# The first norm of the sample rows on ScalarE: row squares and row scaling moved off VectorE

## Chip, cores and metric

The kernel runs on one core of a Trainium2 chip. The metric is device time in microseconds (us), from the start to the end of one execution of the program. The core's engines are TensorE (PE; weight loads are listed as PEld), VectorE (DVE), ScalarE (ACT), GpSimd (POOL) and SyncE (SP), which issues the transfers here. Each engine works through a queue of its own in order; they wait for each other by semaphores.

## What is computed

The reference is one layer of an encoder with two parallel head groups, run for a prompt of 512 rows and a sample of 1024 rows with the same weights, 1024 channels wide, all in float32:

```python
h = _rmsnorm(x, norm_attn_g[l])            # the norm that is changed, for the sample's rows
z = h @ w_in[l]                            # 1024 -> 1792: q, k, v of the attention, ca, cb of the convolution
a_out = _window_attn(q, k, v, bias, band, attn_sink[l])      # 8 heads, 2 kv heads, |q-k| <= 128
c = ca * jax.nn.sigmoid(cb)
c = _dwconv(c, conv_dw_w[l], conv_dw_b[l])                   # 31 taps
c = jax.nn.silu(_layernorm(c, conv_ln_g[l], conv_ln_b[l]))
x = x + jnp.concatenate([a_out, c], axis=-1) @ w_out[l]
h = _rmsnorm(x, norm_ffn_g[l])
u = _dwconv(h @ w_up[l], ffn_dw_w[l], ffn_dw_b[l])           # 3 taps
x = x + (jax.nn.silu(u[..., :D_FF]) * u[..., D_FF:]) @ w_down[l]
# _rmsnorm(x, g): x * rsqrt(mean(x * x over the channels) + 1e-6) * g; once more at the end
```

## The kernel before

**Tiling.** Rows are handled in tiles of 128 rows by 1024 channels, four of which make a block of 512 rows: block 0 is the prompt, blocks 1 and 2 are the sample. Every matmul operand is split into a rounded part and a rest (`split`, lines 140 to 145: a cast on ScalarE, line 143, and a subtraction on GpSimd, line 144), and each product is three matmuls (lines 250, 251, 253; line 257 is the late form of the third).

**The first norm.** `make_h1(nt)` takes the four x tiles of block `nt`, calls `norm_in_place` on each, and then `transposed`. `norm_in_place` sums the squares of each row, alternately on ScalarE (even tiles, line 196) and on VectorE (odd tiles, line 198), lets GpSimd make the factor rsqrt(mean + eps) of it (`rstd_of`, lines 127 and 128), and scales the tile in place on VectorE (line 201). `transposed` has TensorE transpose the four tiles chunk by chunk (line 209) into a PSUM bank; ScalarE takes the rounded part out of it (line 211) and VectorE the rest (line 212), after which the bank is free.

**What runs beside it.** The prompt's projections (`step(i, 0)`) go through 14 chunks of 128 columns of `w_in`; for each, `want_raw` loads the weights (line 137) and `want_w` splits them. `evac` takes the result out of its bank: for a `cb` chunk a tanh on ScalarE (line 314), for the `ca` chunk after it a multiplication with that tanh on VectorE (line 323). A finished pair gives one channel group of the convolution, `conv_items`: a first tap on VectorE (line 289), 26 more for the prompt (line 293), and four taps on ScalarE (lines 282 and 285) that GpSimd adds up (line 286); line 301 joins the two. The small constants come in through TensorE transposes and VectorE copies (lines 176, 416 to 420); the bias table goes from VectorE (line 434) to DRAM (lines 436 and 438).

`make_h1(0)` runs first of all. `make_h1(1)` is queued in `side` at the fourth chunk and `make_h1(2)` at the sixth; `tick` takes a step from `side` at a pace while the prompt's projections go on.

**What sets the order.** The order of the Python calls gives priorities only. The scheduler of the Tile framework deals the instructions of each engine into a queue by a simulated timeline, so a change of one instruction's engine can move others. `tc.issue_after(marks[...])` keeps block 1's norm behind the last bank evacuation of block 0. From the sample's feed-forward part on (line 1202), TensorE's order is the written one.

**Buffers.** `sb` hands out named slots of SBUF (15 of 4 KiB, `q`, for x tiles and weights), `banks` eight PSUM banks `a`, `u`, `b`, `c`. A transfer into a slot waits until the last reader of the slot is done.

Of the kernel before, what the change touches and what calls it, by code (L numbers as in the profile page):

```python
# [12 lines left out]
AF = mybir.ActivationFunctionType  # L13
# [83 lines left out]
def tile_hybrid_encoder(ctx: ExitStack, tc: tile.TileContext, xs, rel_bias, norm_attn_g, w_in,  # L97
                        attn_sink, conv_dw_w, conv_dw_b, conv_ln_g, conv_ln_b, w_out, norm_ffn_g,
                        w_up, ffn_dw_w, ffn_dw_b, w_down, norm_final_g, onehot, outs):
    nc = tc.nc  # L100
# [11 lines left out]
    def sm(n):  # L112
        return sb.tile([n])
# [12 lines left out]
    def rstd_of(ss, n, out):  # L126
        nc.gpsimd.tensor_scalar(out, ss, 1.0 / n, EPS, op0=ALU.mult, op1=ALU.add)
        nc.gpsimd.tensor_tensor(out, out, nhalf[:], op=ALU.pow)
# [60 lines left out]
    lng, lnb, fb = vecs[:, 20:24], vecs[:, 24:28], vecs[:, 28:72]  # L189


    def norm_in_place(x, k):
        ss, rs = sm(1), sm(1)
        junk = sb.tile([D], BF16, 2)
        if k % 2 == 0:
            nc.scalar.activation(junk[:], x[:], AF.Square, accum_out=ss[:])
        else:
            nc.vector.tensor_tensor_reduce(out=junk[:], in0=x[:], in1=x[:], scale=1.0, scalar=0.0,
                                           op0=ALU.mult, op1=ALU.add, accum_out=ss[:])
        rstd_of(ss[:], D, rs[:])  # L200
        nc.vector.tensor_scalar_mul(x[:], x[:], rs[:])

    marks = []

    def transposed(xn, g, h):
        for kc in range(KC):
            pt = bank("turn")
            for i in range(4):
                nc.tensor.transpose(pt[:, i * P:(i + 1) * P], xn[i][:, kc * P:(kc + 1) * P], ident[:])
            hi, lo = sb.tile([NT], F32R), sb.tile([NT], F32R)  # L210
            ia = nc.scalar.activation(hi[:], pt[:], AF.Identity, scale=g[:, kc:kc + 1])
            iv = nc.vector.scalar_tensor_tensor(lo[:], pt[:], g[:, kc:kc + 1], hi[:].bitcast(F32),  # L212
                                                op0=ALU.mult, op1=ALU.subtract)
            h.append((hi, lo))
            marks.append((ia.ins, iv.ins))
            yield 0.0
# [154 lines left out]
    def make_h1(nt):  # L371
        xt = xq.pop(nt)
        for k, x in enumerate(xt):
            if nt == 1:
                with tc.issue_after(marks[KC - 1][0]), tc.issue_after(marks[KC - 1][1]):
                    norm_in_place(x, k)
            else:
                norm_in_place(x, k)
            if nt:
                yield 0.0  # L380
        h1[nt] = []
        yield from transposed(xt, gA, h1[nt])
# [12 lines left out]
    for _ in make_h1(0):  # L395
        pass
# [45 lines left out]
    for i in range(npr):  # L442
        if i == 3:
            side.append(make_h1(1))
        if i == 5:
            xq[2] = [load_x(GR[1], 4 + i) for i in range(4)]
            side.append(make_h1(2))
        if i == 1:
            constants()
            bbd = bias_to_dram()  # L450
        want_raw(i + 2)
        want_w(i + 1)
        step(i, 0)
        ws.pop(i)
# [1115 lines left out]
```

## Time and profile before

| | us |
|---|---|
| median of three runs | 1566.0 (1565.88 to 1571.18) |
| the profiled execution | 1563.92 |
| its span, first to last instruction | 1562.1 |
| TensorE busy | 1519.2 |
| VectorE busy | 1200.5 |
| ScalarE busy | 799.2 |
| GpSimd busy | 729.5 |

The mean granted TensorE clock of that execution is 0.998. Busy times are sums over one engine; matmuls overlap in their pipeline, so a stretch in which TensorE is listed as fully busy is one without a gap. In the rows of the timeline the first number is the start and the second the duration; what stands in brackets is the time that the engine was idle before the row, and the instruction that ended it. Tile names carry the slot's letter: `q<-q` on line 201 is an x tile scaled in place.

### The profile page before, as it was taken

The numbers are of one execution on the slowest core, as the hardware profiler recorded it, in microseconds if no ns is written. First come the engines' busy times: TensorE is split into PE (matmuls) and PEld (weight loads), VectorE is DVE, ScalarE is ACT, GpSimd is POOL, SyncE is SP. The second block draws the span as 40 slices with busy tenths as digits, with TensorE's granted clock in tenths as the row PEclk, the third lists the DMA queues.
The fourth block names the chain that finished last, engine by engine and source line by source line (L and its number), as shares of the span: only waits on it lengthen the run. The fifth ranks groups of instructions, "written<-read, shape, count | busy, mean of one in ns | idle before, by whom it ended". The sixth has DMA issues, their size and how long they took to land. (4 is left out here: it accounts for less than half of the span.)

```text
span 1562.1 us, 20200 instructions
## 1 busy us (share of the span) xinstructions
PE 1519.2 (97%) x6909; PEld 1234.5 (79%) x6909; DVE 1200.5 (77%) x1731; ACT 799.2 (51%) x1426; POOL 729.5 (47%) x559
## 2 busy tenths in 40 slices
PE   8899899999998999999999999999999999999998
PEld 6787788887886778888877887888888878788886
DVE  7999868638989996756675768777777777877795
ACT  4634566335565655656554455444444445544364
POOL 7651344238576676656653324555555554000135
PEclk9999999999999999999999999999999999999999
DMA  7573246446331333333657222333333332694642
GB/s 229 157 201 95 87 118 165 130 133 166 108 117 64 108 108 109 99 97 95 212 164 230 82 68 78 111 102 101 101 102 102 101 102 101 206 354 144 219 142 108
DMA packets 209771, 207.62 MB, mean 133 GB/s; under 512 B 11156, under 2 KB 150748, under 8 KB 209541
## 3 DMA queue, kind: packets, MB, share of 16 engines
q1 hardware_dynamic: 209669, 206.35, 42.0%
q8 instruction: 54, 0.88, 0.2%
q14 instruction: 48, 0.39, 0.1%
HBM read 158.84 MB, written 48.51 MB: 133 GB/s over the span
## 5 line engine op out<-in xcount | busy, mean ns | idle before, releaser
L144 POOL TENSOR_TENSOR q<-q,q 128x1024 fp32r<-128x1024 f32 x72 | 175.0, 2436 | 68.8 <-ACT q L143 33.8
L921 POOL TENSOR_TENSOR q<-q,q 128x512 fp32r<-128x512 f32 x82 | 114.0, 1401 | 155.9 <-ACT q L1031 151.4
L250 PE MATMUL u<-h,q 128*128 128x512 f32 x400 | 158.5, 396 | 3.6 <-DVE h L775 2.8
L251 PE MATMUL u<-h,q 128*128 128x512 f32 x400 | 158.6, 396 | 0.6 <-DVE h L212 0.6
L253 PE MATMUL u<-h,q 128*128 128x512 f32 x384 | 151.9, 396 | 2.2 <-POOL q L144 2.2
L1045 PE MATMUL w<-h,q 128*128 128x512 f32 x372 | 147.4, 396 | 3.1 <-ACT h L1126 1.7
L1047 PE MATMUL w<-h,q 128*128 128x512 f32 x372 | 145.9, 392 | 0.6 <-POOL q L921 0.6
L293 DVE SCALAR_TENSOR_TENSOR c<-c,cvw,c 128x512 f32<-128x512 f32 x184 | 138.1, 750 | 2.4
L1046 PE MATMUL w<-h,q 128*128 128x512 f32 x350 | 137.6, 393 | 0.0
L143 ACT CAST q<-q 128x1024 fp32r<-128x1024 f32 x72 | 75.6, 1050 | 77.5 <-POOL q L144 44.6
L918 POOL TENSOR_TENSOR q<-q,q 128x1024 f32<-128x1024 f32 x8 | 23.8, 2989 | 182.9 <-DVE q L918 171.2
L250 PE MATMUL b<-h,q 128*128 128x512 f32 x256 | 102.1, 399 | 2.9 <-DVE d L323 2.9
L1354 PE MATMUL w<-h,h 128*128 128x512 f32 x264 | 103.8, 393 | 0.0
L1356 PE MATMUL w<-h,h 128*128 128x512 f32 x264 | 103.6, 392 | 0.0
L921 DVE TENSOR_TENSOR h<-h,h 128x512 fp32r<-128x512 f32 (+1 forms) x128 | 92.3, 764 | 11.4 <-ACT h L925 9.2
L251 PE MATMUL b<-h,q 128*128 128x512 f32 x256 | 100.7, 393 | 0.0
L253 PE MATMUL b<-h,q 128*128 128x512 f32 x256 | 100.5, 393 | 0.0
L1355 PE MATMUL w<-h,h 128*128 128x512 f32 x244 | 95.9, 393 | 0.0
L921 POOL TENSOR_TENSOR c<-q,c 128x512 fp32r<-128x512 f32 x46 | 71.0, 1557 | 51.8 <-ACT c L1031 51.8
L250 PEld LDWEIGHTS u<-h,q 128*128 128x128 f32 x400 | 75.6, 189 | 20.4 <-DVE h L775 3.3
L925 ACT CAST h<-h 128x512 fp32r<-128x512 f32 x101 | 58.7, 618 | 59.4 <-DVE h L921 27.0
L251 PEld LDWEIGHTS u<-h,q 128*128 128x128 f32 x400 | 75.5, 189 | 16.4 <-DVE h L212 1.6
(457 smaller groups left out, 4278.8 us busy)
## 6 DMA issues: line engine op xcount, KB each, us to landing
q<-in_w_up SPq DMA_DIRECT2D x88, 512.0 KB
h<-in_w_down SPq DMA_DIRECT2D x90, 256.0 KB
ga<-q SPq DMA_DIRECT2D x64, 256.0 KB
h<-ga SPq DMA_DIRECT2D x57, 256.0 KB
q<-in_w_in SPq DMA_DIRECT2D x28, 512.0 KB
q<-in_x_sample SPq DMA_DIRECT2D x15, 512.0 KB
h<-qsd SPq DMA_DIRECT2D x24, 256.0 KB
q<-ga SPq DMA_DIRECT2D x20, 256.0 KB
```

Source lines behind the costliest of these rows:

```text
L144: (nc.vector if dve else nc.gpsimd).tensor_tensor(lo[:], raw[:], hi[:].bitcast(F32), op=ALU.subtract)
L250: nc.tensor.matmul(out, whi[:, kc, :], hi[:], start=(kc == 0), stop=False)
L251: nc.tensor.matmul(out, whi[:, kc, :], lo[:], start=False, stop=False)
L253: nc.tensor.matmul(out, wlo[:, kc, :], hi[:], start=False, stop=(kc == KC - 1))
L293: nc.vector.scalar_tensor_tensor(acc[:], src(t), w(t), acc[:], op0=ALU.mult, op1=ALU.add)
L921: (eng or nc.vector).tensor_tensor(out, a, b, op=ALU.subtract)
L1045: nc.tensor.matmul(out, whi[:, s], hi[:], start=(start and c == 0), stop=False, **go)
L1046: nc.tensor.matmul(out, whi[:, s], lo[:], start=False, stop=False, **go)
L1047: nc.tensor.matmul(out, wlo[:, s], hi[:], start=False, stop=(stop and c == 3), **go)
L1354: nc.tensor.matmul(out, sh[:, c], th[:], start=(p == 0), stop=False)
L1355: nc.tensor.matmul(out, sh[:, c], tl[:], start=False, stop=False)
L1356: nc.tensor.matmul(out, sl[:, c], th[:], start=False, stop=(p == NPAIR - 1))
```

## The change

For the sample's blocks (`nt` 1 and 2) all four squares of a block are ScalarE activations, and the scaling of each tile is a ScalarE activation with the row factor as its scale. The prompt's block (`nt` 0) keeps both engines and the scaling on VectorE. The reduction's scratch tile, the row factor on GpSimd, the transposes and the loads are as they were. In numbers: four squares and eight scalings move from VectorE to ScalarE.

```diff
-    def norm_in_place(x, k):
+    def norm_in_place(x, k, first):
         ss, rs = sm(1), sm(1)
         junk = sb.tile([D], BF16, 2)
-        if k % 2 == 0:
+        if k % 2 == 0 or not first:
             nc.scalar.activation(junk[:], x[:], AF.Square, accum_out=ss[:])
         else:
             nc.vector.tensor_tensor_reduce(out=junk[:], in0=x[:], in1=x[:], scale=1.0, scalar=0.0,
                                            op0=ALU.mult, op1=ALU.add, accum_out=ss[:])
         rstd_of(ss[:], D, rs[:])
-        nc.vector.tensor_scalar_mul(x[:], x[:], rs[:])
+        if first:
+            nc.vector.tensor_scalar_mul(x[:], x[:], rs[:])
+        else:
+            nc.scalar.activation(x[:], x[:], AF.Identity, scale=rs[:])
...
             if nt == 1:
                 with tc.issue_after(marks[KC - 1][0]), tc.issue_after(marks[KC - 1][1]):
-                    norm_in_place(x, k)
+                    norm_in_place(x, k, False)
             else:
-                norm_in_place(x, k)
+                norm_in_place(x, k, nt == 0)
```

## The prediction

> **What bounds the kernel.** I read the page's busy times first, then a table of stretches, then TensorE's timeline in the one stretch where it idles early, then the queues of those that it waits for. The first two lines are the page's; the rest is the table (stretch, its length, us busy on PE, PEld, DVE, ACT, POOL, then TensorE's granted clock, DMA share, GB/s).
>
> ```profile
> span 1562.1 us, 20200 instructions
> PE 1519.2 (97%) x6909; PEld 1234.5 (79%) x6909; DVE 1200.5 (77%) x1731; ACT 799.2 (51%) x1426; POOL 729.5 (47%) x559
> ...
> 20.00:40.00 20.00, 20.00 (x87) 15.23 (x86) 18.70 (x23) 7.50 (x10) 17.72 (x13) 1.00 0.57 163
> 40.00:60.00 20.00, 16.32 (x87) 13.01 (x86) 19.61 (x29) 14.52 (x24) 13.11 (x17) 1.00 0.57 187
> ...
> 180.00:340.00 160.00, 160.00 (x747) 131.84 (x746) 106.75 (x186) 73.24 (x142) 52.24 (x45) 1.00 0.42 116
> ```
>
> TensorE is the bound: it idles for 1562.1 − 1519.2 = 42.9 us in all, so a change that leaves its matmuls alone cannot bring more. In the stage of the sample's first norm (20 to 62 us) VectorE is full (18.70 and 19.61 of 20). TensorE's idle stretches there, from its timeline (start, duration, line; in brackets the idle time before it and its releaser):
>
> ```profile
> 48.40 0.39 PE L253 MATMUL b<-h,q 128*128 128x512 f32 x1
> 48.63 0.60 PE L209 MATMUL u<-ident,q 128*128 128x128 f32 x4
> 52.15 0.50 PE L250 MATMUL b<-h,q 128*128 128x512 f32 x1 [2.92 <-DVE d L323]
> ...
> 54.80 0.66 PE L209 MATMUL a<-ident,q 128*128 128x128 f32 x4 [0.76 <-DVE h L212]
> ...
> 62.09 0.50 PE L253 MATMUL u<-h,q 128*128 128x512 f32 x1 [1.24 <-POOL q L144]
> ```
>
> 2.92 + 0.76 + 1.24 = 4.92 us is what the stage has to give. Ahead of the two VectorE releasers stand, in their queue:
>
> ```profile
> 27.99 3.56 DVE L201 TENSOR_SCALAR q<-q,s 128x1024 f32<-128x1024 f32 x2 [0.72 <-POOL s L128]
> ...
> 32.67 4.14 DVE L420 TENSOR_SCALAR fw<-fw 128x22 f32<-128x22 f32 x3
> 36.72 2.95 DVE L201 TENSOR_SCALAR q<-q,s 128x1024 f32<-128x1024 f32 x1
> 39.59 0.68 DVE L323 SCALAR_TENSOR_TENSOR d<-h,u 128x512 f32<-128x512 f32 x1
> ...
> 41.16 7.88 DVE L293 SCALAR_TENSOR_TENSOR c<-d,cvw,c 128x512 f32<-128x512 f32 x10
> 48.95 1.22 DVE L198 CUSTOM_DVE_ANT_0 h<-q 128x1024 bf16<-128x1024 f32 x1
> ...
> 51.41 0.68 DVE L323 SCALAR_TENSOR_TENSOR d<-h,b 128x512 f32<-128x512 f32 x1
> ...
> 53.33 0.75 DVE L201 TENSOR_SCALAR q<-q,s 128x1024 f32<-128x1024 f32 x1
> 53.99 0.75 DVE L212 SCALAR_TENSOR_TENSOR h<-a,vecs,h 128x512 fp32r<-128x512 f32 x1
> ```
>
> **Removed from VectorE.** Four of the six squares (L198) and eight of the twelve scalings (L201); the group rows give min/median/max in ns:
>
> ```profile
> L198 DVE CUSTOM_DVE_ANT_0 h<-q x6: 1215/1224/3309, 6.1 to 54.7; 128x1024 bf16<-128x1024 f32 x6
> ```
> ```profile
> L201 DVE TENSOR_SCALAR q<-q,s x12: 749/753/2954, 7.8 to 60.2; 128x1024 f32<-128x1024 f32 x12
> ```
>
> By the medians 4 × 1.22 + 8 × 0.75 = 10.9 us go. In the trace some hold the queue longer: one scaling 2.95, and the three multiplications of 22 columns (L420) between them 4.14. GpSimd runs its weight splits at those times:
>
> ```profile
> 31.93 7.19 POOL L144 TENSOR_TENSOR q<-q,q 128x1024 fp32r<-128x1024 f32 x3
> ...
> 59.67 5.18 POOL L144 TENSOR_TENSOR q<-q,q 128x1024 fp32r<-128x1024 f32 x2
> ```
>
> The Trainium skill's page "SBUF — State Buffer", section "Who interferes with whom", gives a cause: VectorE and GpSimd lock one shared port pair against each other, and ScalarE waits for nobody. By it the relief is more than the medians say; the trace agrees (2954 against 749 ns). The sum below needs only the 10.9, which already exceeds 4.92.
>
> **Step by step.** In the changed program's order the constants' copies and L420 follow the prompt's norm at once, ahead of GpSimd's run of L144, and the first L323 comes next. Its input is complete when the second projection ends on TensorE, and L434, which stands just before it, needs only L432:
>
> ```profile
> 24.86 1.02 PE L432 MATMUL a<-h,rb 33*8 33x512 f32 x2
> ...
> 28.67 1.98 PE L257 MATMUL u<-h,q 128*128 128x512 f32 x8
> ```
>
> So the first L323 can start at 31 instead of 39.59. Twelve L293 follow, 7.88 / 10 = 0.79 us each, and the queue reaches the second L323 near 42 instead of 51.41. Bounds: taken locally only (the square at 48.95 and one scaling behind it go, 1.22 + 0.75 = 1.97), L323 would come at 49.44 and end at 50.12, still after TensorE asks for the bank (48.63 + 0.60 = 49.23), and 2.0 of the 2.92 us is the gain. With the lead of 8 us all 2.92 goes. I take the latter, since the need beyond the local gain is only 0.9. The wait of 1.24 is for the split at 59.67, which GpSimd does after the rstd of the last square; in the changed order this split stands ahead of that rstd, so the wait goes whatever the square costs on ScalarE.
>
> **Added on ScalarE.** Four squares and eight scalings. A scaling of 1024 SBUF columns by a per-row factor does not occur there; the nearest rows:
>
> ```profile
> L1420 ACT ACTIVATE q<-q,s 128x512 f32<-128x512 f32 x6 | 4.3, 722 | 3.8 <-POOL s L1416 3.8
> L1162 ACT ACTIVATE q<-w,vecs,fw 128x1024 f32<-128x1024 f32 x26 | 31.4, 1207 | 25.5 <-PE w L1047 23.1 <-DMA ga<-q 0.9 <-DVE w L918 0.8
> ```
>
> It lies between the square's 1.06 (below: no factor) and 1.21 (one factor more, from PSUM); I take 1.15. Together 4 × 1.06 + 8 × 1.15 = 13.4 us, on an engine with 12.5 us free from 20 to 40 and 5.5 from 40 to 60. It fits; what counts is who is queued behind. ScalarE's queue now:
>
> ```profile
> 42.77 0.58 ACT L314 ACTIVATE h<-u 128x512 f32<-128x512 f32 x1
> 45.86 1.05 ACT L143 CAST q<-q 128x1024 fp32r<-128x1024 f32 x1 [2.50 <-DMA q<-in_w_in]
> 47.08 1.06 ACT L196 ACTIVATE h<-q 128x1024 bf16<-128x1024 f32 x1 [0.18 <-DMA q<-in_x_sample]
> ...
> 49.68 1.06 ACT L196 ACTIVATE h<-q 128x1024 bf16<-128x1024 f32 x1 [1.45 <-DMA q<-in_x_sample]
> 50.74 0.67 ACT L211 ACTIVATE h<-a,vecs 128x512 fp32r<-128x512 f32 x1
> 52.13 0.72 ACT L282 ACTIVATE h<-d,cvw 128x512 f32<-128x512 f32 x1 [0.73 <-DVE d L323]
> 52.76 1.93 ACT L285 ACTIVATE h<-d,cvw 128x512 f32<-128x512 f32 x3
> ```
>
> In the changed order the cast that waits for a weight load stands ahead of that tanh (L314), which the second L323 reads; and three squares, two scalings, L282 and three L285 stand ahead of the first L211, which with its L212 frees the bank of the 0.76 wait. The loads decide. SyncE issues them behind the bias table's store, and that waits for L434 on VectorE:
>
> ```profile
> 32.77 0.30 SPq L436 DMA_DIRECT2D bvd<-h  x1
> ...
> 34.93 0.52 SPq L137 DMA_DIRECT2D q<-in_w_in  x1
> ```
>
> With L434 done near 27 the store leaves 5 us earlier, and the weight load as soon as its buffer is free, when the second projection has ended: 31, that is 4 us earlier. Then the cast runs at 42, the tanh ends at 43.5 and the second L323 starts there, well before 49. The norm's pieces (3 × 1.06 + 2 × 1.15, loads 4 us earlier too) end at 49.2, L282 and the L285 at 51.9, L211 at 52.6, L212 at 53.3. TensorE wants that bank 19 matmuls after 49.23, 0.23 us each (48.63 − 48.40): 53.6. Just in time, so I count the 0.76 as gone.
>
> GpSimd keeps all its L127 and L128, and SyncE issues the same loads in nearly the same order. After the stage TensorE has no idle time from 180 to 340, so a lead is kept. VectorE arrives at the prompt's attention with more lead than TensorE has gained; of its short waits there (the 0.84 below is the first) I count 0.7 as gone, an estimate. Sum: −4.92 − 0.7 = −5.6 us. The profiled execution took 1563.9 (1.8 around the span) and would take 1558.3; the median of the runs, 1566.0, is 2.1 above it, so I forecast 1560.4.
>
> **Rivals.** Idle times of TensorE that a new order can deal anew, and the table's row after the last of them:
>
> ```profile
> 153.37 0.50 PE L561 MATMUL a<-q,h 128*128 128x512 f32 x1 [0.84 <-DVE q L549]
> ...
> 470.13 0.62 PE L502 MATMUL a<-q,h 128*128 128x384 f32 x2 [0.95 <-DVE h L549]
> 473.50 0.61 PE L250 MATMUL u<-h,q 128*128 128x512 f32 x1 [2.75 <-DVE h L775]
> ```
> ```profile
> 473.00:478.00 5.00, 4.50 (x13) 3.55 (x14) 5.00 (x9) 1.57 (x2) 0.00 (x0) 0.66 0.00 0
> ```
>
> (1) *More than the stage.* At 469 two waits (3.70 us) and the clock of 0.66 over 5 us behind them (1.7 us) make 5.4 us in one place. In the changed order six down-projection matmuls are dealt in between. If that fills it: 1560.4 − 5.4 = 1555.0. Against it: the waits are VectorE's, and its work there is the same. Chance 0.24.
>
> (2) *ScalarE becomes the late one.* If the loads land as before (45.86, 49.68), the tanh ends at 47.4, the norm's pieces at 53, the L285 at 55.7, L212 at 57.1, where TensorE wants the bank at 53.6: 3.5 us come back, and about 1 more at the next two transposes. Net −1.1: 1564.9. The Trainium skill's page "ScalarE: Activation LUTs", section "Rules for kernel authors", speaks for this one: multiplications belong on VectorE. The trace agrees for the single instruction (1.06 to 1.21 against 0.75). Chance 0.18.
>
> (3) *Slower.* The list scheduler deals the queues anew up to the sample's attention (360 to 620), where VectorE is a second bound. Each place like the one at 469 costs 5.4 us; from two more on it decides: 1560.4 + 10.8 = 1571.2, three 1576.6. Against it: the trace has one such place now, and the 2.92 wait alone left the clock at 1.00. Chance 0.10.
>
> **Numbers.** The forecast's case has 0.48. A difference of 0.5% (7.8 us) is about what a measurement of this kernel can tell from no change. Faster by more (under 1558.2): rival 1, and 0.07 of the forecast's own spread: 0.31. Slower by more (over 1573.8): three places, 0.06. Within: 0.63. The range 1553.5 to 1567.5 takes in rivals 1 and 2 and the local bound of the 2.92 (0.9 us less), and leaves out rival 3 and the far side of rival 1.
>
> **What would show it.** Right: no TensorE idle time over 1 us from 40 to 65, the first L323 near 31, the second before 49, L420 under 1 us for all three. Wrong: TensorE waiting from 45 to 60 for L211, L212 or L314, with L143 ahead of the tanh waiting for a DMA past 45; or new waits with a lowered clock from 100 to 620.

## The result and the profile after: 1.5% slower

| | before | after |
|---|---|---|
| median of the runs, us (6 each) | 1565.5 | 1588.3 (1583.3 to 1593.0) |
| ratio, 95% interval | | 1.0148 (1.0121 to 1.0175) |
| the profiled execution, us | 1563.9 | 1583.3 |

The profiled execution is the changed kernel's fastest run, so its trace shows 19.4 of the 22.8 us by which the medians differ (1583.3 − 1563.9 and 1588.3 − 1565.5). Lines from 205 on are three higher than before (L253 for L250, L326 for L323). The page's busy line first:

```profile
span 1581.6 us, 20207 instructions
PE 1527.6 (97%) x6909; PEld 1239.1 (78%) x6909; DVE 1177.0 (74%) x1715; ACT 810.3 (51%) x1442; POOL 721.2 (46%) x559
```

VectorE lost 23.5 us of work and ScalarE got 11.1. TensorE has the same 6909 matmuls, but is listed 8.4 us longer busy (1527.6 − 1519.2) and idles 11.1 us more (54.0 against 42.9). More busy time for the same matmuls goes with a lowered clock: the granted clock of the whole execution is 0.992, against 0.998 before.

The stage of the norm itself did what was forecast. Its stretches (the columns are those of the prediction's table):

```profile
20.00:40.00 20.00, 20.00 (x89) 15.33 (x89) 12.95 (x26) 15.98 (x23) 18.23 (x16) 1.00 0.81 229
40.00:60.00 20.00, 20.00 (x104) 16.58 (x103) 15.72 (x24) 18.39 (x29) 10.12 (x16) 1.00 0.55 185
60.00:80.00 20.00, 20.00 (x105) 16.63 (x104) 18.97 (x29) 11.96 (x17) 15.55 (x9) 1.00 0.51 141
180.00:340.00 160.00, 156.44 (x707) 126.97 (x707) 104.15 (x175) 70.23 (x139) 48.44 (x40) 0.98 0.39 106
```

TensorE has no gap from 20 to 80, and VectorE fell from 18.70 and 19.61 to 12.95 and 15.72. The last row is the surprise: where TensorE had been busy for 160.00 of 160 with 747 matmuls, it now idles 3.6 us, gets through 707, and has a clock of 0.98.

To see where time goes, each matmul of the changed kernel was matched with the same matmul before (same line and tile names, the n-th with the n-th). The median lag by stretches of the trace before (a matmul that the new order moves counts with its own shift, so between 220 and 360 and near 590 the columns jump):

| stretch before, us | 200–220 | 280–320 | 340–360 | 380–440 | 500–520 | 580–600 | 660–740 | 860–900 |
|---|---|---|---|---|---|---|---|---|
| lag after, us | −5.8 | +8.6 | +2.7 | +12.4 | +13.4 | +19.9 | +18.1 | +19.6 |

So 5.8 us are gained, and from 220 to 660 some 24 us are lost; behind that little happens. TensorE's rows with its larger waits there (in brackets the idle time and its releaser):

```profile
241.86 0.49 PE L563 MATMUL a<-q,h 128*128 128x512 f32 x1 [0.67 <-ACT q L551]
243.18 0.50 PE L564 MATMUL a<-q,h 128*128 128x512 f32 x1 [0.82 <-DVE q L552]
...
245.45 0.79 PE L253 MATMUL b<-h,q 128*128 128x512 f32 x1 [1.31 <-DVE q L331]
...
372.86 1.62 PE L505 MATMUL a<-q,h 128*128 128x256 f32 x6 [7.30 <-DMA q<-ksd]
...
486.54 0.60 PE L816 MATMUL b<-h,h 128*128 128x512 f32 x1 [3.55 <-DVE q L819]
...
605.25 0.50 PE L564 MATMUL a<-h,h 128*128 128x512 f32 x1 [1.79 <-DVE h L552]
```

The four places, as stretches of 20 us, after and then before:

```profile
240.00:260.00 20.00, 17.17 (x69) 13.01 (x68) 17.77 (x33) 11.00 (x26) 5.33 (x5) 0.83 0.50 133
...
360.00:380.00 20.00, 11.66 (x43) 8.80 (x44) 13.62 (x21) 8.58 (x13) 8.97 (x6) 0.74 0.62 155
480.00:500.00 20.00, 15.27 (x60) 11.97 (x59) 18.22 (x29) 9.15 (x15) 6.16 (x5) 0.91 0.10 32
600.00:620.00 20.00, 17.32 (x70) 13.24 (x70) 12.13 (x24) 10.33 (x23) 12.60 (x11) 0.91 0.17 54
```
```profile
240.00:260.00 20.00, 20.00 (x97) 16.44 (x96) 18.15 (x34) 12.72 (x29) 6.64 (x6) 1.00 0.68 176
...
360.00:380.00 20.00, 18.40 (x82) 14.39 (x81) 17.73 (x25) 10.00 (x14) 13.44 (x9) 1.00 0.52 144
480.00:500.00 20.00, 19.50 (x92) 15.75 (x90) 16.60 (x32) 11.12 (x23) 12.43 (x9) 1.00 0.27 87
600.00:620.00 20.00, 19.44 (x90) 15.75 (x89) 13.19 (x28) 10.40 (x22) 13.93 (x9) 1.00 0.44 142
```

Read the bracket after the busy time (matmuls that ran) and the clock behind POOL: 69, 43, 60 and 70 matmuls at 0.74 to 0.91, against 97, 82, 92 and 90 at 1.00. None of the four places touches the norm; the nearest lies 180 us behind it. The third is not a new loss in full: with a lag of 12.4 us, its waits at 482.5 (1.18 us) and 486.5 (3.55) stand at the same point of the program as the old place at 469 to 477 (3.70 us of waits, with a lowered clock behind them), whose two matmuls no longer wait. The lag grows only from 12.4 to 13.4 us there.

What differs is the order. The two programs hold the same instructions, apart from the twelve that moved; of TensorE's 6908 listed places 2628 hold another instruction. By line and tile names alone, without buffer numbers, the two traces differ in at least 2163 of TensorE's places, 693 of VectorE's and 122 of SyncE's transfers. At 240, for example, the prompt's attention transposes its probabilities (L546, after: L549), ScalarE and VectorE take them out of the bank, and TensorE multiplies the result (L560, after: L563). Before, nine projection matmuls stand between the two and fill the time:

```profile
242.97 0.38 PE L546 MATMUL a<-ident,q 128*128 128x128 f32 x2
243.10 0.47 PE L250 MATMUL b<-h,q 128*128 128x512 f32 x1
...
245.28 0.39 PE L560 MATMUL a<-q,h 128*128 128x512 f32 x1
```

In the new order none does: the last transposes start at 240.80, and the next matmul is the one at 241.86 with the wait of 0.67 us shown above.

### The profile page after: what moved, and what is told of

Its sections match the earlier page's. It is cut to its first block, busy times and chain, and to the rows that moved or that the text cites. A ratio compares the mean times of both kernels' runs of the same rounds, so it can differ in the third digit from the quotient of the medians.

```text
span 1581.6 us, 20207 instructions
## 1 busy us (share of the span) xinstructions
PE 1527.6 (97%) x6909; PEld 1239.1 (78%) x6909; DVE 1177.0 (74%) x1715; ACT 810.3 (51%) x1442; POOL 721.2 (46%) x559
## 5 line engine op out<-in xcount | busy, mean ns | idle before, releaser
L253 PE MATMUL u<-h,q 128*128 128x512 f32 x400 | 159.8, 399 | 3.9 <-DVE h L778 1.6
L253 PE MATMUL b<-h,q 128*128 128x512 f32 x256 | 102.3, 401 | 1.3 <-DVE q L331 1.3
L253 PEld LDWEIGHTS u<-h,q 128*128 128x128 f32 x400 | 76.3, 191 | 22.7 <-DVE h L778 3.2
L928 ACT CAST h<-h 128x512 fp32r<-128x512 f32 x101 | 58.9, 618 | 59.1 <-DVE h L924 26.9
```

The source lines that it names most:

```text
L253: nc.tensor.matmul(out, whi[:, kc, :], hi[:], start=(kc == 0), stop=False)
```

## The experiments

In most of them the order of the queues is listed instead of dealt. Such a kernel holds a table of instruction positions and ties each instruction to its predecessor in the table, by an edge that sets the order of issue only and adds no wait:

```diff
+def _pin(nc, tc):
...
+        for _ in range(d.popleft()):          # one engine's list
+            at += d.popleft()
+            ins = traced[at]
+            if prev is not None:
...
+                tc.add_manual_dep(ins, prev.name, mybir.DependencyInfo(
+                    mybir.DependencyClass.NoSync, mybir.DependencyReason.DATA), reason="pin")
+            prev = ins
...
+    _pin(nc, tc)                               # last line of the kernel
```

The table shifts the line numbers of these kernels by some 50 to 110. Ratios are against the kernel before, run beside each (its medians: 1563.4 to 1565.9).

| run | what | median, us | ratio (95%) |
|---|---|---|---|
| 1 | change, old order | 1561.2 | 0.9971 (0.9960–0.9983) |
| 2 | no change, new order | 1605.4 | 1.0249 (1.0229–1.0270) |
| 3 | scalings only, dealt freely | 1567.2 | 1.0005 (0.9994–1.0016) |
| 4 | squares only, dealt freely | 1592.8 | 1.0172 (1.0149–1.0195) |
| 5 | change, new order to 200 us, then old | 1560.5 | 0.9977 (0.9963–0.9992) |
| 6 | the same, to 300 us | 1567.2 | 1.0015 (1.0001–1.0029) |
| 7 | the same, to 430 us | 1577.7 | 1.0090 (1.0059–1.0120) |
| 8 | change, TensorE's order alone as before | 1559.0 | 0.9964 (0.9949–0.9978) |
| 9 | one square moved, dealt freely | 1591.1 | 1.0176 (1.0158–1.0193) |
| 10 | one scaling moved, dealt freely | 1584.9 | 1.0138 (1.0123–1.0153) |
| 11 | run 8, taps later at 469 | 1557.8 | 0.9964 (0.9951–0.9977) |
| 12 | before, taps later at 469 | 1562.6 | 0.9996 (0.9980–1.0011) |
| 13 | run 7's kind, to 620 us | 1581.2 | 1.0107 (1.0087–1.0126) |
| 14 | run 8, all taps 15 us later | 1566.7 | 1.0022 (0.9997–1.0047) |
| 15 | change, new order, scores later at 372 | 1587.4 | 1.0144 (1.0119–1.0169) |

### Work or order (runs 1 and 2)

Run 1 lists every queue as before in the changed kernel; run 2 lists every queue as in the changed kernel, with the norm left on VectorE.

> The changed kernel, with the issue order of every engine's queue listed as in the kernel before (the twelve moved instructions are left to the scheduler, which puts them at places 14 to 50 of ScalarE's queue). Theory A (the loss is in the order that the scheduler deals, not in the work that moved): the stage of the norm gains 4 to 6 us and nothing is lost later, 1558 to 1563 us, and no idle time of 7.3 us behind the K loads near 370. Theory B (twelve more instructions on ScalarE delay what follows them, whatever the order): the loss stays, 1580 to 1590.

> The kernel before, norm on VectorE as it was, with the issue order of every queue listed as in the changed kernel (the twelve instructions left to the scheduler on VectorE). Theory A: the loss comes with the order although no work has moved, and the 5 us of the norm's stage are missing as well: 1588 to 1595 us, with lowered clock at several places from 240 to 610. Theory B: 1563 to 1569.

This settles that the loss comes with the order. The change without the new order gains 4.7 us; the new order without the change loses 39.6, even more than with it. In run 1 matched matmuls are 5.2 us ahead at 178 us and between 4.6 and 6.2 us ahead from there to the end. The same four stretches in run 1, for comparison:

```profile
240.00:260.00 20.00, 20.00 (x100) 16.48 (x99) 18.06 (x31) 13.28 (x29) 11.55 (x9) 1.00 0.76 198
360.00:380.00 20.00, 19.25 (x87) 15.38 (x86) 18.16 (x27) 11.30 (x15) 16.61 (x10) 1.00 0.31 90
480.00:500.00 20.00, 18.95 (x89) 15.24 (x89) 18.22 (x35) 13.04 (x26) 15.08 (x12) 1.00 0.31 93
600.00:620.00 20.00, 20.00 (x97) 16.63 (x96) 12.28 (x25) 9.54 (x20) 9.05 (x6) 1.00 0.32 104
```

Run 2 is 17 us slower than the changed kernel. Between their profiled executions 18.6 us lie in the first 77 us: with the norm on VectorE the new order makes TensorE wait 8.81 us at 40, 2.29 at 67 and 2.24 at 72. At 1605.4 us it lies above theory A's range, which counts 5 us for the norm's stage; behind 77 us the distance stays between 18 and 24 us to the end.

### Halves and single instructions (runs 3, 4, 9 and 10)

```diff
-        if k % 2 == 0:
+        if k % 2 == 0 or act:                       # run 9; run 10: the scaling line likewise
...
-                norm_in_place(x, k)
+                norm_in_place(x, k, nt == 2 and k == 3)      # run 10: k == 0
```

> Half of the change: the eight scalings go to ScalarE, the four squares stay on VectorE. The scheduler deals freely; 600 of TensorE's 6908 places differ from the order before, against 2628 in the changed kernel. Theory A: near the kernel before, 1556 to 1568 us. Theory B: the scalings are 9.2 of the 13.4 us that went to ScalarE, so some two thirds of the loss, 1578 to 1584.

> The other half: the four squares go to ScalarE, the scalings stay on VectorE. 2597 of TensorE's 6908 places differ from the order before, and only 324 from the changed kernel's. Theory A: near the changed kernel, 1580 to 1592 us. Theory B: a third of the loss, 1571 to 1575.

> The kernel before with one single instruction moved: the square of block 2's last tile, on ScalarE in place of VectorE (1.06 us for 1.22). Freely dealt; 2506 of TensorE's 6908 places change, and 329 differ from the changed kernel's. Theory A (the order decides): 1577 to 1592 us. Theory B (what moved decides, a twelfth of it): 1564 to 1567.

> The kernel before with one scaling moved: that of block 2's first tile (0.75 us on VectorE). 2421 of TensorE's 6908 places change, and 799 differ from the changed kernel's. Theory A: the order is a relative of the changed kernel's, 1575 to 1592 us. Theory B: 1564 to 1567.

The size of what moves has nothing to do with the loss: eight scalings cost nothing net, one scaling 21.5 us, one square 27.7, and all four squares 26.9 (run 4, just above theory A's range). Run 9's waits stand where the changed kernel's stand, with their sizes:

```profile
247.42 0.49 PE L560 MATMUL a<-q,h 128*128 128x512 f32 x1 [0.67 <-ACT q L548]
...
251.01 0.80 PE L250 MATMUL b<-h,q 128*128 128x512 f32 x1 [1.30 <-DVE q L328]
...
377.26 1.62 PE L502 MATMUL a<-q,h 128*128 128x256 f32 x6 [6.53 <-DMA q<-ksd]
...
490.07 0.80 PE L813 MATMUL b<-h,h 128*128 128x512 f32 x1 [3.56 <-DVE q L816]
...
609.98 0.50 PE L561 MATMUL a<-h,h 128*128 128x512 f32 x1 [1.78 <-DVE h L549]
```

The same waits come with nearly the same order, 3.5 to 5.6 us later, since the stage's gain is missing. Run 3 is a warning against reading a ratio of 1.00 as "nothing happened": its matched matmuls are 7.1 us ahead of the kernel before at 200 us and 1.5 us behind from 280 to 440. It has the place at 240 too, and not the long wait for the K loads:

```profile
242.20 0.80 PE L253 MATMUL b<-h,q 128*128 128x512 f32 x1 [0.97 <-DVE q L331]
...
368.36 0.95 PE L505 MATMUL a<-q,h 128*128 128x256 f32 x6 [0.66 <-DMA q<-ksd]
```

So 8.6 us went between 220 and 280, more than the whole gain: waits of 0.68, 0.75, 0.97 and, at 257, 1.30 us, with a granted clock of 0.89 from 240 to 260 and 0.94 from 260 to 280. This place doesn't bring the late K loads (the loads of the attention's K) with it.

### Where in the order (runs 5, 6, 7 and 13)

Every queue follows the new order up to a time of TensorE, and the old order for all the rest.

> The changed kernel, every queue in the changed kernel's own order for what is dealt up to TensorE's 200 us, and in the order of the kernel before for all the rest. Theory A1 (each later place costs where it stands): the stage's gain in full and no loss, 1557 to 1561 us. Rival A2 (the early order, with its earlier and differently spaced loads and banks, is what makes all later places late): above 1575.

> The same with the join at TensorE's 300 us, so that the places from 224 to 265 us of the changed kernel (waits of 0.5 to 1.3 us in the prompt's attention, and the lowered clock behind them) are in, those behind them not. Matched matmuls of the changed kernel stand 5 to 9 us behind the kernel before's at 285 to 357. Theory A1: 1570 to 1575 us. Rival A3 (one place, the wait of 7.3 us for the K loads at 372 with its lowered clock, carries the loss and the others give back): 1557 to 1563.

> The same with the join at 430 us: the wait for the K loads is in as well. Matched matmuls are 12.5 us behind there. Theory A1: 1576 to 1581 us, of the 1588 of the whole; what is missing then lies from 430 to 870. Rival A3: 1585 to 1590.

> The changed kernel, every queue in its own new order up to TensorE's 620 us and in the old order behind it. With the join at 430 it took 1577.7 us, the whole new order 1588.3. Theory A1 (the remaining 10 us stand at the waits for VectorE between 480 and 606 and the lowered clock behind them): 1584 to 1590. Rival (they lie behind 620, where 973 of TensorE's places still differ): 1577 to 1581.

Against the runs beside them: −4.4, +2.3, +12.8 and +16.8 us, with +22.8 for the whole. So 6.7 us go between 200 and 300 and 10.5 between 300 and 430, where the waits stand. The 4.0 between 430 and 620 are not clear of noise (the intervals of runs 7 and 13 overlap). Theory A1 holds for runs 5 and 7; run 6 came out below its range and above rival A3's, and run 13 below it too, at the upper end of its rival's. The 6 us left over are not placed: in the two profiled executions the changed kernel is only 0.5 us later than run 13 at 880 us.

### Which queue (run 8)

> The changed kernel with TensorE's issue order alone listed as in the kernel before; the scheduler deals the other four queues freely. They come out near the old ones by themselves (176 of VectorE's 1617 places differ, 12 of SyncE's 697). Theory A4 (TensorE's order is the one that matters, the others follow from it): 1558 to 1563 us. Rival A5 (the loads' and VectorE's order in the first 200 us matter more): 1575 or more.

Listing TensorE's order alone is enough: the scheduler then deals the other queues nearly as before by itself. So no run separates what TensorE's new order costs from what the other queues' new orders cost. This is a version that is faster than both kernels, by 5.9 us against the one before.

### Single places (runs 11, 12, 14 and 15)

In runs 11 and 12 four convolution taps (L293 in the kernel before; the expectation counts five) and one scaling of probabilities go back in VectorE's queue, behind what TensorE waits for at 469. In run 14 the whole stream of taps from 456 us on is listed 15 us later, in run 15 the scores (L505) behind 24 projections:

```diff
-... tap, sums, tap, tap, tap, sum, tap, 1/sum, FFN tap, rest, tap, scaling, FFN tap, rest
+... tap, sums, tap, rest, FFN tap, FFN tap, tap, tap, sum, 1/sum, scaling, rest, tap, tap
```

> The changed kernel in the order of the run with TensorE's old order, every queue listed, with one edit: in VectorE's queue at 462 to 470 us, five convolution taps and a scaling of probabilities go behind the two FFN taps and the subtraction that TensorE waits for there (1.19 and 2.76 us, then 6 matmuls at 0.63 in place of 0.39 us). Theory P (the place costs 5.4 us, as the prediction priced it, and VectorE has slack behind it): 1552 to 1555 us against 1559. Rival (VectorE is full there, so the taps only move the wait to the next place at 497): 1557 to 1560.

> The kernel before in its own order, with the same edit of VectorE's queue and nothing else. Theory P: 1559 to 1562 us, so that this gain and the norm's add up. Rival: 1564 to 1567.

> The changed kernel with TensorE's old order, and VectorE's queue listed with its whole stream of convolution taps, from 456 us to the stream's end near 600, moved back by 15 us, some 6 us of VectorE work, to where VectorE has 5 us in 20 free. The other three queues are dealt freely. Theory F (VectorE is full from 440 to 600, so a repaired place returns 20 us later unless work leaves the stretch): the waits from 470 to 515 (1.19, 2.76, 0.87, 1.24 us and 1.7 us of lowered clock) go, 1551 to 1555 us against 1559. Rival (single late chains from TensorE over ScalarE to VectorE, not VectorE's load): 1558 to 1562.

> The changed kernel in its own new order, every queue listed, with one edit in TensorE's: the six score products that wait 7.30 us for the K loads at 372 go behind the 24 projection matmuls that follow them (24 by 0.23 = 5.5 us). Theory P (this place costs its 7.3 us and 3.4 us of lowered clock by itself): the wait shrinks to about 2 us and the clock stays at 1.00, 1577 to 1581 us against 1588. Rival (the scores' softmax, now 5.5 us later on VectorE, sets the waits from 480 on, and what is gained returns there): 1584 to 1589.

Run 11's TensorE, and its stretches 460 to 500, show why nothing came of it (run 8 had 16.05 and 18.95 busy there):

```profile
491.52 0.68 PE L918 MATMUL b<-h,h 128*128 128x512 f32 x1 [2.35 <-DVE q L921]
493.17 1.01 PE L607 MATMUL a<-q,h 128*128 128x384 f32 x2 [0.97 <-DVE s L610]
```
```profile
460.00:480.00 20.00, 20.00 (x93) 16.39 (x92) 18.99 (x33) 12.13 (x23) 9.45 (x6) 1.00 0.31 92
480.00:500.00 20.00, 16.68 (x69) 13.19 (x68) 18.79 (x31) 13.55 (x27) 18.00 (x13) 0.83 0.24 80
```

The place at 469 is filled. It returns at 491 with 3.3 us of waits and its own lowered clock. Run 11 has the ratio of run 8, as its rival had it; run 12 that of no change, between its two ranges.

Run 14 was to show that VectorE's fullness does this. It doesn't: VectorE falls to 16 to 18 of 20 from 460 to 600, and TensorE waits all the same, elsewhere.

```profile
495.38 0.62 PE L577 MATMUL a<-q,h 128*128 128x384 f32 x2 [1.53 <-DVE s L580]
541.76 0.79 PE L636 MATMUL a<-h,h 128*128 128x512 f32 x1 [3.45 <-DVE h L624]
583.64 0.62 PE L577 MATMUL a<-q,h 128*128 128x384 f32 x2 [2.25 <-DVE s L580]
```

So Theory F falls. Its rival, late single chains, agrees with the new waits but not with the time: 1566.7 us is above both ranges, and 7.7 us above run 8. Since ScalarE's, GpSimd's and SyncE's queues were dealt anew in run 14, it proves neither.

In run 15 the wait for the K loads is gone and the clock stays at 1.00. Where its order is the changed kernel's again (382 us there), its matched matmuls are 7.2 us better off against it than ahead of the edit. Two waits for FFN taps that now come late on VectorE take that back: 4.7 us are left behind the first, 0.2 behind the second, which has a lowered clock after it:

```profile
384.49 0.47 PE L355 MATMUL u<-h,q 128*128 128x512 f32 x1 [2.27 <-DVE h L880]
434.69 0.77 PE L355 MATMUL u<-h,q 128*128 128x512 f32 x1 [2.71 <-DVE h L880]
```

The rival's time held; the return came at 384 and 435, over FFN taps, and not at 480 over the softmax. The late K loads themselves can be followed in the traces of before and after, though no run tried this chain: the last two K loads need the buffer of an x tile, which is free once TensorE has transposed it. The last of those transposes and the loads, before and then after:

```profile
355.92 0.60 PE L209 MATMUL a<-ident,q 128*128 128x128 f32 x4
```
```profile
356.70 1.23 SPq L679 DMA_DIRECT2D q<-ksd  x2
```
```profile
360.88 0.66 PE L212 MATMUL a<-ident,q 128*128 128x128 f32 x4 [0.28 <-DVE h L215]
```
```profile
361.72 1.43 SPq L682 DMA_DIRECT2D q<-ksd  x2
```

They come 5.0 us later, while TensorE runs out of other matmuls at nearly the same time: it waits from 366.3 for 0.6 us before, from 365.6 for 7.3 us after.

## Why the prediction was wrong, step by step

- **The three waits go** (4.92 us): right for the changed kernel, which has no gap from 40 to 80. In run 1, with the old order, two shorter ones stay (0.59 us at 55, 0.73 at 58): its lead is 4.1 us there, and 5.2 only after a wait for a load that is 1.39 us before (at 119) is 0.62. By the medians run 1 gains 4.7 us.
- **VectorE's queue**: right. First L323 forecast near 31, second near 43.5, L420 under 1 us for all three:

```profile
25.53 0.34 DVE L423 TENSOR_SCALAR fw<-fw 128x22 f32<-128x22 f32 x3
...
30.84 0.69 DVE L326 SCALAR_TENSOR_TENSOR d<-h,u 128x512 f32<-128x512 f32 x1 [4.16 <-PE u L260]
...
42.44 0.69 DVE L326 SCALAR_TENSOR_TENSOR d<-h,b 128x512 f32<-128x512 f32 x1 [0.57 <-ACT h L317]
```

- **ScalarE**: right. The cast forecast at 42 and the scaling estimated at 1.15 us:

```profile
40.87 1.05 ACT L143 CAST q<-q 128x1024 fp32r<-128x1024 f32 x1 [4.88 <-DMA q<-in_w_in]
41.82 0.59 ACT L317 ACTIVATE h<-u 128x512 f32<-128x512 f32 x1
```
```profile
L204 ACT ACTIVATE q<-q,s x8: 1137/1164/1192, 26.9 to 56.2; 128x1024 f32<-128x1024 f32 x8
```

  Rival 2 (ScalarE late) did not occur. The rule of the Trainium skill's page "ScalarE: Activation LUTs", section "Rules for kernel authors" (multiplications on VectorE), holds for the single instruction, 1164 against 753 ns, and not for this stage: run 1 gains with them on ScalarE.
- **The 0.7 us of the prompt's attention**: wrong, and small. The wait of 0.84 stayed (0.84 in the changed kernel, 0.83 in run 1). That the lead at 200 is 5.8 us, near the forecast's 5.6, is luck: the matched lead is 5.7 us at 60 to 120, 7.3 at 140, where the wait of 1.39 at 119 is gone, and falls again at a wait for a load at 171, 3.48 us for 1.67 before.
- **"After the stage TensorE has no idle time from 180 to 340, so a lead is kept"**: this step failed. It is true of one order: in run 1 the lead is kept to the end. It was applied to a program whose order behind the stage is another one. There the lead of 5.8 us at 200 is a lag of 18.1 us at 660. The first new place, at 240, lies inside the very stretch that was called safe.
- **Rival 3** named the mechanism (queues dealt anew, waits with a lowered clock) and was given 0.10, because the trace before has one such place. That is no evidence on another order. Its other ground, the clock of 1.00 behind the 2.92 us wait, was the luck of where that wait fell (last section). Its bounds were wrong as well: it began at 240 and not at 360, and two of the places cost 6.7 to 8.6 us (the joins at 200 and 300; run 3) and 10.5 us (the joins at 300 and 430), not 5.4 each.
- **Rival 1** expected the place at 469 to be filled. Its two matmuls no longer wait, but two others do at the same point of the program (482 and 486), for 4.73 us. Runs 11, 12 and 15 show why such a price can't be added up: a place filled by hand came back 10 to 60 us later. Where the 27 us go between the changed kernel in the whole old order (run 1) and in its own, the joins show up to 430 us; why none of the single edits of either order brought a gain stays open beyond that.

## What to carry to other kernels

Where a scheduler deals the queues from a simulated timeline, an edit is two changes: the work that moves, and a new order of everything behind it. Count how many places of the bounding engine's queue differ; if they are thousands, a forecast worked out from the old trace holds only for the stretch in which the order is still the same, and the sign of the rest is open. To measure the work, or to keep its gain, list the bounding engine's order as before: here that turned 22.8 us of loss into 5.9 us of gain.

## What was not expected of the hardware

TensorE's granted clock fell without any long wait. The lowered stretches of all 17 traces last 3.41 us, two or three times that (but for a last one that runs past the program's end), and within a trace they begin whole multiples of 3.41 us apart. So the time can be cut along them. Two such cuts of the changed kernel, two of the kernel before around its wait of 2.92 us, and two of run 12, which has its wait at the same place (2.16 us, starting at 50.6):

```profile
241.04:244.45 3.41, 1.61 (x6) 0.67 (x4) 3.38 (x8) 2.51 (x5) 0.00 (x0) 1.00 0.26 97
244.45:247.86 3.41, 2.41 (x6) 1.92 (x7) 3.38 (x8) 3.10 (x10) 0.00 (x0) 0.50 0.67 166
```
```profile
47.08:50.49 3.41, 2.15 (x13) 1.60 (x11) 3.34 (x6) 1.96 (x3) 0.97 (x3) 1.00 1.08 367
50.49:53.91 3.42, 1.76 (x7) 1.24 (x7) 3.42 (x6) 2.69 (x6) 2.42 (x5) 1.00 0.35 128
```
```profile
49.22:52.63 3.41, 1.39 (x9) 0.93 (x7) 2.97 (x5) 1.72 (x3) 3.03 (x5) 1.00 0.90 282
52.63:56.05 3.42, 3.28 (x8) 2.50 (x9) 3.42 (x6) 3.30 (x6) 2.60 (x3) 0.50 0.02 7
```

The next clock goes by TensorE's busy time within one such cut. Counted over the 17 traces from 30 to 1545 us, starting from a clock of 1.00: each of the 55 cuts with less than 46% busy is followed by a lowered one, of the 38 from 46 to 57% 7 are, and of the 7363 above that none. Waits of 0.67, 0.82 and the first part of one of 1.31 us left 1.61 of 3.41 us, and halved the clock; the 2.92 us were split between two cuts with 2.15 and 1.76 us left, and did not; run 12's shorter wait fell into one cut, left 1.39, and did. Where the cuts fall is not set by the order, which is the same there in run 12 and in the kernel before. So one order can get different clocks: run 13 has the changed kernel's order up to 620 us and a wait of 3.69 us at 171 (the changed kernel 3.48); a cut around it has 1.41 us busy in run 13, and the next a clock of 0.50, while the changed kernel's two cuts have 1.65 and 1.69 and keep 1.00.

The Trainium skill's page "TensorE: Matmul & The Clock Gate", section "Why this matters for your kernels", warns of idle gaps over some 3 us; here shorter ones were enough when several stood together, or when one fell into a single cut.
